# Where x tiles 4 to 7 land, the order of a first stage written out by hand, and context products two tiles later

## The chip, the cores and the metric

The kernel runs on one core of a Trainium2 chip. The metric is the device time of that core in microseconds (us), the median of several runs. The core has a matrix engine (PE, with its weight loads shown apart as PEld), a vector engine (DVE), a scalar engine (ACT), a general engine (POOL) and the queue SP, from which nearly all DMA transfers are issued here. Matmul results are written to PSUM, which this kernel uses as eight banks of 128x512 floats.

## The reference

One layer of an image backbone on 1024 latent tokens (x) and 256 context tokens (ctx), width 1024:

```
shift, scale, gate = adaln(c, w_ada, b_ada);  shift_c, scale_c, _ = adaln(c_ctx, ...)
h  = rmsnorm(x, norm_g)   * (1 + scale)   + shift
hc = rmsnorm(ctx, norm_g) * (1 + scale_c) + shift_c
q, k, v, za, u, bg, cg, zc = split(h @ w_in)          # 8 x 512 columns
kc, vc = split(hc @ w_in[:, 512:1536])
attn = neighbourhood_attention(rms(q), rms(k), v, rms(kc), vc, rpb) * silu(za)
conv = bg * conv3(cg * u) * silu(zc)
out  = x + gate * (concat(attn, conv) @ w_out)
```

All products are formed with an operand split into a high and a low float32r half: high*high, high*low, low*high.

## The kernel before

**Three places.** The kernel has a first stage (in the trace up to about 62 us on PE), a stage of 32 projection tiles (8 for each pair of heads, with context products and turns of the results between them), and then attention and output. The change touches the first stage and the first few tiles of the second.

**The first stage** is a list of short words, `LOADS` (line 36) and `STEPS` (lines 37 to 49), which `do` (line 789) runs in the order written. Up to the attention stage every engine's instructions, and SP's DMA issues, are chained in program order (`ordered`, lines 56 to 76), so a word that has to wait holds up all later words on its own engine. Since all of these instructions are issued in the helper, the profile gives nearly all of them line 71, and they are told apart by tile names. The words, with the engine that they run on:

- SP, loads: `s` a slab of the modulation weights (1 MB, three buffers), `t` a 128x512 piece of x transposed (256 KB; `t0k` for tokens 0 to 511 in three buffers, `t1k` for tokens 512 to 1023 in eight), `c` a weight chunk of the convolution columns and `q` one of the first pair of heads (192 KB; both in the five `wr` buffers), `x` a tile of 128 rows of x and `n` one of the two tiles of context tokens (512 KB), `e` context tokens transposed (`xc`), `g` the gains and the table for the rotations.
- PE: `pr k` the products of slab k with the conditioning vectors (64 small matmuls), `fc h k i` one of the three products of chunk k with token half h (three 128x512 matmuls, tile `acc`), `wb k` the products of the shift with chunk k (8 matmuls, tile `shifted`), `T t` two transposes of x tile t, `Rt g` transposes of the row sums of group g (into `tr`), `fill n` n matmuls with zeros.
- ACT: `ch`/`qh` the high half of a chunk, `sq t` the sum of squares of tile t, `p k` and `hi h k` high halves of the scaled tokens, `sh`, and `R g` the copy of `tr` into a spread row `rs`.
- DVE: `tp`, `ab` (modulation of slab k), `cl`/`ql` low halves of chunks, `m k`, `u h k` (scaling), `lo h k` low halves, `rp` (normalises an `acc` bank), `rg` (rotation tables), `wt` (transposes `shifted`), and with POOL `root g` (the inverse root of a group's sums; group 0 is x tiles 0 to 3, group 1 is 4 to 7, group 2 the context tiles).
- `conv` runs the next part of the first convolution group: a copy on ACT, a product on DVE, and the second time two more ACT additions.

There are 48 `fc` words; a slab's `pr k` comes ahead of `tp k`, `ab k`, and these ahead of `p1k`, `u0k` and all that follows for that k.

**x tiles** (`load_x`, line 564). Tiles 0 to 3 go into two places of the pool that later holds the h tiles 6 and 7 (`place(6)`, `place(7)`, two tiles in each). Tiles 4 to 7 and the two context tiles share two buffers `xn`.

**After the list** the first convolution group is finished on DVE (four taps and two gains, tile `cv`). Then the `rope` table goes out to `rope_d` and back (SP), POOL clears `gacc` (in the buffer that the taps read), SP loads one row into it, and then loads the first unit weights `uraw`. These four DMA steps are in this order on SP.

**The projection loop** (line 1190) runs n over the tiles. In turn n: PE does tile n (24 matmuls, tile `pacc`, banks in the order S, S, O, O of line 308, so tile 4 needs the bank of tile 0). Turn n measures tile n-1 (`head_scale`: ACT `sq`, DVE `ss`, POOL `ss`; `put_v`: ACT `vs`), and normalises tile n-2 (`rms_normed`: ACT `qn`, the last reader of that bank). `rotated` follows on DVE; every second turn PE turns two tiles (`turn_qk`: `trA`, `trB`). `CONTEXT` (line 50), 16 words that make the context operand `hc` on DVE and ACT, is issued in turn 0, right behind tile 0. At the end of turn 0 ACT makes the high halves `uh` of the unit weights (`do_acts`). At the end of turn `at` (line 1194), PE does the context products (`cacc`, 32 matmuls, in the two U banks); `ctx_sums` reads them in turn at+1, `normed_ctx` reads them for the last time in turn at+2 (ACT `kn`, `vs`), `turn_kc` is issued in turn at+3. From turn 5 on, 12 matmuls of the first unit (tile `pu`) follow behind each projection tile; their accumulator takes the first U bank too (`unit`, line 370: the tile is taken when its first matmul is issued).

Of the kernel before, what the change touches and what calls it, by code (L numbers as in the profile page):

```python
# [10 lines left out]
F32 = mybir.dt.float32  # L11
# [8 lines left out]
P = 128  # L20
D = 1024
# [4 lines left out]
NB = 8  # L26
NH, HD = 8, 64
NPAIR = NH // 2
# [4 lines left out]
TICKS = [2, 3, 3, 4, 4, 4, 4, 1] + [4, 4, 4, 1] + [4, 4, 4, 2] + [4, 4, 4, 1] + 3 * [4, 4, 3, 1] + [3, 2, 3, 1]  # L33
EPS = 1e-6

LOADS = "s0 t10 c0 x0 s1 t11 c1 x2 x3 x1 s2 c2 t12 t02"
STEPS = [
# [11 lines left out]
]  # L49
CONTEXT = "Hi0 Hi1 Lo0 Lo1 Hi2 Hi3 Lo2 Lo3 Hi4 Hi5 Lo4 Lo5 Hi6 Hi7 Lo6 Lo7"  # L50

# [4 lines left out]
def body(tc, es, x, xb, xt, cb_, ct, w_mod, w_gate, b_ada, w_grp, w_col, q_g, k_g, bias, w_out, vecs, cst, out):  # L56
# [86 lines left out]
    c2 = cp.tile([P, KT, 2], F32, name="c2")  # L143
# [10 lines left out]
    def place(k, shape, dtype, name):  # L154

        return hpool.tile(shape, dtype, name=name, tag=f"h{k}")

    def more_h(ks):
        for k in ks:
            t = place(k, [P, 2, T], F32R, f"h{k}")  # L160
            hh.append(t[:, 0])
            hl.append(t[:, 1])
# [10 lines left out]
    def chunk_load(col, k):  # L173
        raw = wpp.tile([P, 3, P], F32, name="wr", tag="wr", bufs=5)
        sp.dma_start(raw[:].rearrange("p a n -> p (a n)"), w_grp[NPAIR if col == CU else (col - CQ) // P, k])
        return raw
# [29 lines left out]
    def next_vs():  # L206
        vss.append(vss.pop(0))
        return vss[-1]
# [8 lines left out]
    def normed(qn, ps, scale, n):  # L217
        for h in range(n):
            cols = slice(h * HD, (h + 1) * HD)
            act.activation(qn[:, cols], ps[:, cols], AF.Identity, scale=scale[:, h:h + 1])  # L220
# [6 lines left out]
    def rms_normed(pp, ps, scale):  # L227

        qn = pp.tile([P, 256], F32, name="qn", tag="qn", bufs=3)
        normed(qn, ps, scale, 4)  # L230
        return qn
# [83 lines left out]
    def unit_load(col):  # L315
        raws = []
        for q in range(2):
            raws.append(uw.tile([P, 4, P], F32, name="uraw", tag="uraw", bufs=2))
            sp.dma_start(raws[q], w_col[col // P, :, 4 * q:4 * q + 4])
        return raws  # L320
# [85 lines left out]
    def z_col(f):  # L406
        return CZA + f * P if f < 4 else CZC + (f - 4) * P
# [154 lines left out]
    xn, xh, xc, slabs, mods, rows, chunks, pair = {}, {}, {}, {}, {}, {}, {}, []  # L562

    def load_x(t):
        if t < 4:
            if t % 2 == 0:
                pair.append(place(6 + t // 2, [P, 2, D], F32, "xn"))
            xn[t] = pair[t // 2][:, t % 2]
        else:
            xn[t] = xp.tile([P, D], F32, name="xn", tag="xn", bufs=2)[:]  # L570
        sp.dma_start(xn[t], xb[t * P:(t + 1) * P] if t < NB else cb_[(t - NB) * P:(t - NB + 1) * P])
# [189 lines left out]
    def keep_clock(n, late=False):  # L761

        v = zeros[:].rearrange("p (o n) -> p o n", o=1).broadcast_to([P, 4, P]) if late else warm
        ps = acc0[1][0][:].rearrange("p (a n) -> p a n", a=4) if late else acc0[1][0]
        for _ in range(n):
            pe.matmul(ps, zeros if late else warm[:, :P], v, start=True, stop=True)
# [22 lines left out]
    def do(steps):  # L789
        for word in steps.split():  # L790
            name = word.rstrip("0123456789")
            at = word[len(name):]
            does[name](*([int(at)] if name in ("warm", "fill") else map(int, at)))
# [9 lines left out]
    more_h(range(6))  # L803
    do(LOADS)
    keep_clock(6)
# [380 lines left out]
    def flush():  # L1186
        while stores:
            stores.pop(0)()

    for n in range(NT + 3):  # L1190


        p, t = divmod(n, NB)
        at = 2 if p < NPAIR - 1 else 0
        if t and p + 1 < NPAIR:
            raws.append(chunk_load(CQ + (p + 1) * P, t))
        if n == 0:
            loaded[z_col(4)] = unit_load(z_col(4))
        if n == NT - 8:
            loaded[z_col(0)] = unit_load(z_col(0))  # L1200
        if 9 <= n <= KT + 8:
            gate.load(n - 9)
        if n == NT - 3:
            act.activation(few[:, 5:6], ones, AF.Exp)
        if n == NT - 6:
            heads[0].masks()
            heads[0].load_k()
        if n == NT - 5:
            heads[0].load_q()
        flush()  # L1210
        blocks = divmod(n - 6, 5)
        if 6 <= n < 26 and blocks[1] == 0:
            load_blocks(blocks[0])
        if n == 24:
            sp.dma_start(ab[:, :, 0], g_d.rearrange("o (t p) -> p (o t)", p=P))

        if t == 0 and 0 < n < NT:
            nxt += map(chunk_split, raws)
            ch, nxt, raws = nxt, [], []
        if t == 0 and p + 1 < NPAIR:  # L1220
            raws.append(chunk_load(CQ + (p + 1) * P, 0))
        if n == 0:
            next(group0)
        if n == NT - 4:
            next(fill)
        if n < NT:
            tiles[n] = proj_tile(ch, t)
            if n == 0:
                do(CONTEXT)
        else:  # L1230
            for _ in range((4, 3, 1)[n - NT]):
                next(fill)
        if 5 <= n < 9:
            for _ in range(2):
                next(group0)
        if n == 9:
            for _ in group0:
                pass
        if 0 < n <= NT:
            scales[n - 1] = head_scale(pp, tiles[n - 1], 4)  # L1240
            if n % 2:
                vs = next_vs()
            put_v(vs, (n - 1) % 2, tiles[n - 1][:, 256:384])
            if n % 2 == 0:
                q, r = divmod(n - 1, NB)
                spill_v(q, r - 1, vs)
        if t == at + 1 and n < NT:
            ctx_sums(pp, cacc)
            cscales = [head_scale(pp, a, 2) for a in cacc]

        if 1 < n <= NT + 1:
            m, r = n - 2, (n - 2) % NB
            qn = rms_normed(pp, tiles[m], scales.pop(m))
        while waiting:
            waiting.pop(0)()
        if 4 <= t and p + 1 < NPAIR:
            nxt.append(chunk_split(raws.pop(0)))
        if 1 < n <= NT + 1:
            tiles[m] = rotated(pp, rope, qn, r)
        if t == at + 2 and n < NT:  # L1260
            kc = normed_ctx(pp, cacc, cscales)
        do_dves()
        if 6 <= n < 26 and blocks[1] in (2, 3):
            add_blocks(*blocks)
        if 10 <= n < KT + 10:
            gate.add(n - 10)
        do_acts()

        if n == KT + 11:
            gate.split()  # L1270
        if n == KT + 13:
            gate.sum()
        if t == at and n < NT:
            cacc = ctx_products(ch)
        if n % 2 == 0 and n >= 4:
            waiting.append(turn_qk(pp, (n - 4) // NB, [tiles.pop(n - 4), tiles.pop(n - 3)], (n - 4) % NB))
        if t == at + 3 and n < NT:
            waiting.append(turn_kc(pp, p, *kc))
# [74 lines left out]
    with sbuf("att") as ap, psum("psb") as psb:  # L1353
# [6 lines left out]
        for n in range(len(TICKS)):  # L1360
# [11 lines left out]
            if ready:  # L1372
                p = ready.pop()
# [83 lines left out]
    def four(tags):  # L1457
        return [bank("pout", tag) for tag in tags]
# [44 lines left out]
    m12, m22 = zip(*[(residual(c, 1), residual(4 + c, 1)) for c in every_tile])  # L1503
    load_left(6, "B")
    m11 = [residual(c, 0) for c in every_tile]
# [19 lines left out]
    c5 = four("OOUU")  # L1525
# [29 lines left out]
    c3 = four("OOUU")  # L1555
# [84 lines left out]
```

## Time and profile before

| what | us |
|---|---|
| median of 3 runs (lowest, highest) | 602.52 (602.45, 603.16) |
| the profiled execution's own time | 602.64 |
| its span, first to last instruction | 600.8 |
| PE busy in the span | 579.1 |
| DVE busy | 445.8 |
| ACT busy | 290.2 |

Every instruction row of the profile has its start in us, its length in us, the engine, the line (almost always the helper's line 71), the operation, and the tiles as output<-inputs; a row with x24 stands for 24 merged instructions. In square brackets stands the idle time of the engine just before the row, and what released it. Rows of the stretches (windows) have, for each engine, its busy time, the number of instructions, and then the granted clock of PE (PEclk, 1.00 is full speed), the busy share of the DMA engines and GB/s.

### The profile page before, as it was taken

How to read it: one execution, taken by the hardware profiler on the slowest of the kernel's cores; microseconds unless marked ns; L12 is line 12 of the kernel's file. 1: busy time of each engine (PE TensorE's matmuls, PEld its weight loads, DVE VectorE, ACT ScalarE, POOL GpSimd, SP SyncE). 2: the span in 40 equal slices, each digit the busy share in tenths (PEclk: the TensorE clock that was granted, in tenths of full speed). 3: DMA queues.
4: the chain of work that ended last, by engine and by line, in shares of the span. 5: the costliest groups of instructions: out<-in, count | busy, mean ns of one | idle time of the engine just before them, and what ended most of it. 6: DMA issues, size and time to landing. Idle time of an engine off the chain costs nothing.

```text
span 600.8 us, 10008 instructions
## 1 busy us (share of the span) xinstructions
PE 579.1 (96%) x3574; PEld 484.9 (81%) x3574; DVE 445.8 (74%) x894; ACT 290.2 (48%) x671; POOL 58.0 (10%) x83
## 2 busy tenths in 40 slices
PE   7899569999999999999999999999999999999998
PEld 4677469999999999988887777878787876888886
DVE  2556887356995765546898968898988887999952
ACT  4564546342553545543464446465644735643320
POOL 0000104112322223200000000000000001100000
PEclk9999879999999999999999999999999999999999
DMA  8988251537896879394616374736576363682632
GB/s 312 415 328 319 110 215 51 190 124 243 271 317 214 280 233 341 117 353 170 215 60 247 129 254 125 283 115 233 196 261 223 116 228 114 192 308 72 209 121 90
DMA packets 66678, 126.14 MB, mean 210 GB/s; under 512 B 8713, under 2 KB 27649, under 8 KB 64324
## 3 DMA queue, kind: packets, MB, share of 16 engines
q1 hardware_dynamic: 66244, 124.70, 59.3%
q0 software_dynamic: 384, 0.81, 0.5%
q8 instruction: 28, 0.46, 0.3%
q14 instruction: 22, 0.18, 0.1%
HBM read 92.38 MB, written 33.10 MB: 209 GB/s over the span
## 4 chain that ended last, share of the span: by engine, by line
PE 82%; DMA 8%; DVE 6%; ACT 2%; SPq 1%; issue 1%; DVEq 0%; ACTq 0%
PE pu L71 27%; PE pacc L71 19%; PE pout L71 13%; PE po L71 5%; PE cacc L71 4%; PE acc L71 3%; PE pss L71 3%; PE pc L71 2%; DMA slab<-in_w_mod 2%; PE pmx L71 2%; DMA xn<-in_cb 1%; PE trA L71 1%; DMA wr<-in_w_grp 1%; PE tr L71 1%; DMA y_d<-tb 1%
## 5 line engine op out<-in xcount | busy, mean ns | idle before, releaser
L71 PE MATMUL pu<-h,uh 128*128 128x512 f32 x544 | 174.3, 402 | 0.0
L71 PE MATMUL pacc<-w,h 128*128 128x384 f32 x768 | 141.9, 342 | 8.5 <-ACT rs L71 7.6
L71 PEld LDWEIGHTS pacc<-w,h 128*128 128x128 f32 x768 | 135.5, 192 | 9.3 <-ACT rs L71 7.9
L71 PEld LDWEIGHTS pu<-h,uh 128*128 128x128 f32 x544 | 97.4, 189 | 18.3 <-issue 1.2
L71 PE MATMUL pu<-h,ul 128*128 128x512 f32 x272 | 106.5, 392 | 0.0
L71 PE MATMUL pout<-right,left 128*128 128x512 f32 (+2 forms) x348 | 77.0, 383 | 0.0
L71 PEld LDWEIGHTS pout<-right,left 128*128 128x128 f32 x348 | 64.4, 188 | 12.7
L71 PEld LDWEIGHTS pu<-h,ul 128*128 128x128 f32 x272 | 51.1, 188 | 11.4
L71 POOL TENSOR_TENSOR ss<-ss,few 128x4 f32<-128x4 f32 (+1 forms) x40 | 41.3, 1033 | 128.1 <-DVE ss L71 127.7
L71 ACT COPY sc<-pc 128x512 f32<-128x512 f32 x32 | 18.7, 587 | 45.5 <-PE pc L71 45.5
L71 PE MATMUL acc<-h,w 128*128 128x512 f32 x144 | 36.4, 401 | 1.8 <-ACT h L71 1.7
L71 ACT ACTIVATE sq<-pacc 128x256 f32<-128x256 f32 x32 | 12.3, 385 | 48.7 <-PE pacc L71 48.2
L71 ACT ACTIVATE sc<-sc 128x512 f32<-128x512 f32 x32 | 20.3, 633 | 30.0 <-DVE sc L71 29.8
L71 PEld LDWEIGHTS acc<-h,w 128*128 128x128 f32 x144 | 26.0, 188 | 9.2 <-ACT h L71 2.6
L71 DVE TENSOR_TENSOR sum<-sum,sb 128x372 f32<-128x372 f32 (+2 forms) x64 | 31.1, 485 | 2.7
L71 DVE SCALAR_TENSOR_TENSOR m<-pout,ab,m 128x512 f32<-128x512 f32 (+2 forms) x34 | 22.9, 721 | 13.0 <-PE pout L71 12.9
L71 ACT ACTIVATE qn<-pacc,ss 128x64 f32<-128x64 f32 x128 | 30.0, 330 | 4.0 <-PE trA L71 2.5
L71 DVE TENSOR_TENSOR mx<-mx,sb 128x372 f32<-128x372 f32 (+2 forms) x64 | 30.9, 483 | 1.4
L71 DVE TENSOR_REDUCE ss<-sq 128x4 f32<-128x260 f32 (+1 forms) x40 | 15.7, 392 | 21.8 <-ACT sq L71 21.8
L71 DVE TENSOR_TENSOR sb<-pss,bt 128x192 f32<-128x192 f32 (+3 forms) x48 | 27.7, 604 | 4.2 <-PE pss L71 4.2
L71 DVE TENSOR_TENSOR ul<-uraw,uh 128x512 fp32r<-128x512 f32 x34 | 23.1, 685 | 10.0 <-ACT uh L71 10.0
L71 DVE TENSOR_TENSOR sb<-sb,mg 128x744 f32<-128x744 f32 (+2 forms) x32 | 26.7, 834 | 0.0
(154 smaller groups left out, 862.6 us busy)
## 6 DMA issues: line engine op xcount, KB each, us to landing
uraw<-in_w_col SPq DMA_DIRECT2D x34, 256.0 KB, 3.5
slab<-in_w_mod SPq DMA_DIRECT2D x8, 1024.0 KB, 10.3
q_d<-qs SPq DMA_DIRECT2D x32, 256.0 KB, 5.0
k_s<-k_d SPq DMA_DIRECT2D x8, 1024.0 KB
q_s<-q_d SPq DMA_DIRECT2D x16, 512.0 KB, 4.5
wr<-in_w_grp SPq DMA_DIRECT2D x40, 192.0 KB, 4.1
bt<-in_rpb SPq DMA_DIRECT2D x8, 564.0 KB, 8.3
xn<-in_xb SPq DMA_DIRECT2D x8, 512.0 KB
```

Of the source, the lines that this page charges most:

```text
L71: i = emit(*a, **kw)
```

## The change

- `load_x`: x tiles 4 to 7 go to the same two places as tiles 0 to 3 (tile 4 where tile 0 was, and so on). The two `xn` buffers are left to the context tiles alone.
- `LOADS` and `STEPS` have the same words, except that the zero matmuls are 1, 2 and 4 in place of 2 and 5, in another order. Among the differences: x0 to x3 are loaded behind the first two slabs; x4 and x5 are loaded around slab 4, x6 and x7 ahead of slab 5; the context tiles (`n0 n1`) are loaded ahead of slab 7, where they stood behind all slabs; `sq8 sq9 root2` come ahead of `pr7`, and `Rt2` and `R2`, which were among the last four words, stand well before the end of the list; `rg2 rg1` are the list's last words.
- `CONTEXT` is issued in turn 2, behind `rms_normed` of tile 0, and no longer in turn 0.
- For the first pair of heads the context products come at the end of turn 4 (behind tile 4) and no longer of turn 2. The other pairs keep theirs. With it `ctx_sums`, `normed_ctx` and `turn_kc` go to turns 5, 6 and 7.

```diff
-LOADS = "s0 t10 c0 x0 s1 t11 c1 x2 x3 x1 s2 c2 t12 t02"
+LOADS = "s0 t10 c0 s1 t11 c1 x0 x1 x2 x3 s2 c2 t12 t02"
 STEPS = [
-    "ch0 pr0 s3 t13 c3 t03 t14 c4 t04 tp0 ab0 p10 cl0 sh0 sq0 fc101 fc100 m10 fc102 pr1 s4 x4 x5 T0 ch1 wb0 tp1",
-    "ab1 cl1 p11 sh1 m11 fill2 fc110 sq2 sq3 fc111 fc112 sq1 root0 wb1 T3 ch2 T2 fill5 pr2 s5 tp2 ab2 cl2 sh2 p12",
-    "m12 T1 more Rt0 wb2 R0 fc120 fc121 v00 fc122 hi00 v01 u00 hi01 pr3 lo00 u01 lo01 u02 t05 t15 c5 fc000 fc002",
-    "fc010 tp3 hi02 ab3 fc001 ch3 fc012 p13 fc011 lo02 cl3 fc020 sh3 u03 fc022 hi03 ch4 fc021 m13 fc132 pr4 cl4",
-    "tp4 fc131 sq4 x6 ab4 lo03 fc130 u04 sh4 p14 fc031 fc140 sq5 x7 t16 s6 c6 t06 s7 t17 c7 t07 hi04 fc032 lo04",
-    "ch5 fc141 sq6 fc030 cl5 pr5 fc042 tp5 fc041 fc040 sh5 ab5 wb3 q0 p15 u05 fc151 hi05 sq7 m14 ch6 fc050 root1",
-    "fc150 lo05 m15 fc142 cl6 pr6 tp6 ab6 fc152 sh6 p16 u06 wb5 wb4 q1 q2 g0 n0 n1 m16 hi06 fc051 fc052 ch7 lo06",
-    "pr7 fc162 qh0 qh1 cl7 tp7 fc160 ql0 ab7 qh2 Rt1 fc161 ql1 p17 u07 sh7 wb6 q3 R1 hi07 ql2 u10 fc060 sq8 fc171",
-    "wb7 q4 q5 q7 q6 e0 e1 e2 e3 lo07 u11 fc062 hi10 m17 fc061 fc072 qh3 fc170 sq9 wt ql3 fc071 lo10 qh4 fc172",
-    "hi11 u12 ql4 rp0 root2 qh5 fc070 qh6 ql6 qh7 ql5 ql7 hi12 lo12 lo11 conv0 rp1 u13 u14 hi13 hi14 rg3 lo13 u15",
-    "lo14 hi15 u16 rg0 lo15 rp2 u17 rg2 rg1 hi17 conv0 lo17 Rt2 hi16 R2 lo16",
+    "pr0 s3 t13 c3 ch0 tp0 ab0 cl0 p10 m10 fc101 fc100 sh0 ch1 pr1 tp1 sh1 ab1 wb0 cl1 fc102 p11 m11 sq0 sq1",
+    "fill1 fc110 fc111 fc112 sq2 T1 fill2 T2 T0 x4 s4 t03 x5 t04 x6 c4 t14 sq3 ch2 fill4 pr2 root0 tp2 sh2 ab2",
+    "cl2 p12 wb1 Rt0 m12 T3 x7 s5 R0 v00 u00 wb2 hi00 v01 fc121 ch3 fc120 hi01 fc122 pr3 fc001 lo00 u01 sq4 tp3",
+    "fc000 sh3 lo01 fc002 u02 t05 t15 c5 s6 t16 c6 fc010 fc012 fc011 ab3 hi02 p13 fc020 lo02 fc022 m13 fc021 u03",
+    "t06 n0 n1 hi03 ch4 pr4 s7 c7 t17 cl3 tp4 lo03 fc130 sh4 fc132 ab4 fc030 p14 u04 t07 hi04 sq5 cl4 fc031 fc131",
+    "fc032 sq7 fc140 lo04 sq6 more m14 ch5 fc042 fc041 root1 pr5 fc141 tp5 sh5 fc142 wb3 q0 ab5 u05 p15 hi05 wb4",
+    "q2 cl5 pr6 m15 lo05 fc051 tp6 ch6 ab6 fc151 fc052 fc152 u06 sh6 p16 sq8 fc150 sq9 fc040 m16 fc160 fc050 hi06",
+    "cl6 wb5 q1 root2 pr7 fc161 ch7 lo06 tp7 ab7 sh7 Rt1 cl7 u07 p17 m17 qh0 fc162 wb7 wb6 q3 q4 qh2 R1 ql0 q5 g0",
+    "fc060 fc062 fc171 ql2 q6 u10 u12 qh1 ql1 q7 e0 e1 e2 e3 hi07 fc170 Rt2 lo07 fc172 fc061 fc070 hi10 fc071",
+    "lo10 qh3 ql3 qh5 qh4 ql4 R2 u11 qh6 ql5 hi12 ql6 hi11 qh7 fc072 lo12 wt ql7 lo11 rg0 u13 hi13 conv0 rp0 u14",
+    "hi14 rp1 lo13 u15 rp2 lo14 hi15 conv0 lo15 u16 u17 rg3 hi16 hi17 lo16 lo17 rg2 rg1",
 ]
...
-        if t < 4:
+        if t < NB:
             if t % 2 == 0:
-                pair.append(place(6 + t // 2, [P, 2, D], F32, "xn"))
+                pair.append(place(6 + t // 2 % 2, [P, 2, D], F32, "xn"))
...
-        at = 2 if p < NPAIR - 1 else 0
+        at = (4, 2, 2, 0, 0)[p]
...
             tiles[n] = proj_tile(ch, t)
-            if n == 0:
-                do(CONTEXT)
...
             qn = rms_normed(pp, tiles[m], scales.pop(m))
+        if n == 2:
+            do(CONTEXT)
```

## The prediction

> **What bounds the kernel now.** I read the page's engine table first, then PE's waits, then the timeline of each engine up to 112 us.
>
> ```profile
> PE 579.1 (96%) x3574; PEld 484.9 (81%) x3574; DVE 445.8 (74%) x894; ACT 290.2 (48%) x671; POOL 58.0 (10%) x83
> PE pacc L71 <- ACT rs L71: 7.6, 1, 7.6
> PE tr L71 <- POOL sums L71: 4.7, 1, 4.7
> PE tr L71 <- DMA slab<-in_w_mod: 1.0, 1, 1.0
> 50.60 1.10 PE L71 MATMUL tr<-slab,c 128*32 128x64 f32 x64
> 56.53 5.06 PE L71 MATMUL acc<-h,w 128*128 128x512 f32 x21
> 66.30 0.69 PE L71 MATMUL tr<-ci,sums 128*128 128x128 f32 x2 [4.72 <-POOL sums L71]
> 66.64 5.75 PE L71 MATMUL pacc<-w,h 128*128 128x384 f32 x24
> 79.98 10.06 PE L71 MATMUL pacc<-w,h 128*128 128x384 f32 x48 [7.58 <-ACT rs L71]
> 89.88 5.71 PE L71 MATMUL cacc<-w,hc 128*128 128x512 f32 x32
> 103.75 0.27 PE L71 MATMUL trA<-ci,rot 128*128 128x128 f32 x1
> ...
> 104.32 4.43 PE L71 MATMUL pacc<-w,h 128*128 128x384 f32 x24
> 108.59 0.63 PE L71 MATMUL pu<-h,uh 128*128 128x512 f32 x2
> ...
> 111.36 0.38 PE L71 MATMUL trC<-ci,kn 128*128 128x128 f32 x2
> 111.49 4.42 PE L71 MATMUL pacc<-w,h 128*128 128x384 f32 x24
> ...
> 66.00:68.00 2.00, 1.70 (x6) 1.70 (x7) 2.00 (x5) 0.45 (x1) 1.43 (x6) 0.54 0.00 0
> 80.00:82.00 2.00, 2.00 (x6) 2.00 (x7) 1.97 (x4) 1.38 (x2) 0.00 (x0) 0.50 0.47 197
> ```
>
> PE is the bound, and its two long idles lie at the seam of the stages: 4.72 us ahead of `Rt2`, and 7.58 us ahead of tile 1, which waits for `R2` to read the bank `tr`. After each the granted clock is about half (0.54, 0.50), so that tile 0 takes 5.75 us and tiles 1 and 2 together 10.06, against 4.43 for tile 5 (4.27 from its start to the first `pu`). That is 1.3 and 1.4 us more: 15.0 us at the seam in all. The page leaves PE 600.8-579.1 = 21.7 us of idle, 12.3 of them here. So what the change is worth is read at one point: **when PE starts tile 6**, now 111.49, or 111.36 (so 2.77 behind the first `pu`) without `trC`, which is issued later in the new order.
>
> **The change part by part.**
>
> *The loads.* x4 to x7 no longer wait for `sq4` and `sq5`, the context tiles come earlier, and slabs 5 and 7 stand behind 1.05 MB more.
>
> ```profile
> 20.00:30.00 10.00, 8.86 (x164) 6.75 (x165) 7.35 (x15) 5.28 (x10) 0.52 (x1) 1.00 1.04 417
> 36.00:38.00 2.00, 2.00 (x11) 1.64 (x10) 1.13 (x2) 2.00 (x4) 0.00 (x0) 1.00 0.64 245
> ...
> 40.00:50.00 10.00, 10.00 (x181) 7.48 (x181) 6.04 (x12) 5.56 (x11) 1.44 (x1) 1.00 0.95 358
> 33.91 4.05 SPq L71 DMA_DIRECT2D xn<-in_xb  x2
> 59.79 1.06 ACT L71 ACTIVATE xn<-xn 128x1024 f32<-128x1024 f32 x1 [3.71 <-DMA xn<-in_cb]
> 62.08 0.56 DVE L71 TENSOR_TENSOR w<-wr,w 128x384 fp32r<-128x384 f32 x1 [3.62 <-ACT w L71]
> ```
>
> The transfers run at some 417 GB/s, with a hole from 36 us on (245) where SP stood 4.05 us at x6 and x7. With the hole filled, the 18.25 MB up to slab 7 land near 49.5 us, before PE gets to `pr7`; I take no loss there, and none at slab 5. If they land 1 us late, `pr7` and all behind it are 1 us late. `sq8` no longer holds ACT for 3.71 us and with it DVE for 3.62: gained on DVE. The order of SP's queue costs something else, below.
>
> *PE's list.* Ahead of `pr7` stand one more `fc` (37 for 36; 5.06/7 = 0.72 us) and behind slab 2, for which PE waits (the row with slab) in both, `wb1` (8 small matmuls, an estimate of 0.4 at most from `pr7`'s 64 in 1.10). So `pr7` starts near 50.60+1.1 = 51.7 and ends at 52.8; the list ends about 62.3, with `Rt2` now inside it. Both idles as they are now go. What is late next?
>
> *DVE to the end of the list.* Behind `pr7` DVE has, by start-to-start steps:
>
> ```profile
> 51.81 0.24 DVE L71 STREAM_TRANSPOSE rw<-tr 128x64 f32<-128x64 f32 x1
> 65.14 1.49 DVE L71 TENSOR_TENSOR w<-wr,w 128x384 fp32r<-128x384 f32 x3
> 66.55 1.47 DVE L71 SCALAR_TENSOR_TENSOR h<-hw,b,h 128x512 fp32r<-128x512 f32 x2
> 76.48 1.29 DVE L71 TENSOR_TENSOR rg<-rw 128x512 f32<-128x512 f32 x2
> 79.06 0.69 DVE L71 TENSOR_TENSOR cu<-acc,ub 128x512 f32<-128x512 f32 x1 [1.29 <-ACT acc L71]
> ```
>
> 9 low chunk halves x 0.47 = 4.2; 9 `u`, 9 `lo` and `m17` x 0.66 = 12.5; 4 `rg`, 3 `rp`, 2 `conv` x 0.6 = 5.4; small ones 0.8: 22.9 us. Without any idle that ends at 75.7. Both `conv` copies stand behind a `hi` on ACT (1.2 us, as in the row at 79.06, and some 0.6), and `q6`, `q7` are issued behind `wb6`, `ql2`, `ql1` and the three `g0` loads, so near 59 us, and hold `ql6` and `ql7` for about 1.7. I take 3.5: **the list ends on DVE at E = 79.2**. With the idle that DVE has now (81.0-51.8-22.4 = 6.8) it would be 82.
>
> `wt` stands late in this list, and I take its bank `shifted` for that of tile 0: tile 0 starts near 64.5, tiles 0 to 3 end near 81.
>
> *Tile 4.* It needs the bank of tile 0, thus `qn` of tile 0 on ACT. Ahead of that in ACT's order stands `uh`, which waits for `uraw`, behind `gacc`, behind the taps. Now this chain is covered by `CONTEXT`, which comes first; the change puts `CONTEXT` behind it.
>
> ```profile
> 77.80 0.33 SPq L71 DMA_DIRECT2D rope_d<-rg  x1
> 81.64 0.32 SPq L71 DMA_DIRECT2D rope<-rope_d  x1
> 80.99 2.98 DVE L71 SCALAR_TENSOR_TENSOR cv<-cu,vecT,cv 128x512 f32<-128x512 f32 x4
> 84.09 0.96 POOL L71 MEMSET gacc<- 128x1024 f32 x1 [16.58 <-DVE cv L71]
> 85.38 0.81 SPq L71 DMA_DIRECT2D uraw<-in_w_col  x2
> DMA to landing us min/median/max: 2.8/2.8/2.8
> 85.09 0.87 DVE L71 SCALAR_TENSOR_TENSOR hw<-xc,ab,rs 128x256 f32<-128x256 f32 x2
> ...
> 91.72 0.88 DVE L71 SCALAR_TENSOR_TENSOR hc<-hw,b,hc 128x256 fp32r<-128x256 f32 x2 [0.18 <-ACT hc L71]
> 91.99 1.13 ACT L71 CAST uh<-uraw 128x512 fp32r<-128x512 f32 x2
> 95.45 0.93 ACT L71 ACTIVATE qn<-pacc,ss 128x64 f32<-128x64 f32 x4 [0.89 <-POOL ss L71]
> ```
>
> From the end of the list on DVE (now 80.99) to `uraw`'s issue is 4.39 us. The second `uraw` half is issued 0.4 later and lands after 2.8: E+7.6; `uh` 0.6; from its end (93.12) to `qn`'s (96.38) 3.26: E+11.5. But `rg1` is the last word now, so the 1 MB `rope` load (3.84 us behind `rope_d`) is issued at E+3.9, straight ahead of `uraw`. Its 1.05 MB at 417 GB/s are 2.5 us; behind these and a landing of 2.8 `uraw`'s second half is there near E+9.2, and `qn` ends at E+13.1. I take that: **tile 4 starts at 92.3**, after 11 us idle. The Trainium skill (DMA: Bandwidth & Descriptors, "Queues, rings and completion order") says that SP's DMAs use one row of rings and are consumed in ring order on each engine, which speaks for 13.1; shared evenly it would be E+11.5 to E+13, 1 us less.
>
> *Tile 4 to tile 6.* Tile 4 at half clock 4.3+1.4; `cacc` 5.6 (`CONTEXT`, 7.5 us from 85.09 to 92.6 now, starts when `qn` does and ends in time); turns 0.6 (103.75 to 104.32); tile 5 4.3: 16.2 us. Then `pu` takes the first U bank, which `cacc` holds until `normed_ctx` in turn 6.
>
> ```profile
> 102.34 0.61 ACT L71 ACTIVATE kn<-cacc,ss 128x64 f32<-128x64 f32 x2
> 102.74 0.36 ACT L71 COPY vs<-cacc 128x128 f32<-128x128 f32 x1
> ```
>
> Now that reader ends at 103.1, 7.5 us behind `cacc` (95.6), and `pu` comes at 108.6: hidden. In the new order ACT must first do `sq` and `vs` of tile 5, `qn` of tile 4 and a weight copy: not before 2.6 us behind tile 5 (rows like these). PE leaves only 0.6+4.3 = 4.9 us behind `cacc`, 7.5-4.9 = 2.6 by the present distance; with ACT's queue behind `CONTEXT` I count 4.7. I take 3.7, with 2.77 for `pu` itself, and no clock loss. The two idles in the first fence say that 4.7 us halves the clock; the Trainium skill (TensorE: Matmul & The Clock Gate, "What's actually happening") gives an idle window of about 3.4 us. By it the 3.7 us would cost up to 1.4 more; PE's waits hold no idle between 1.8 and 4.7 us here.
>
> Sum: 92.3+16.2+3.7+2.8 = 115.0, against 111.36: **3.6 us later**. Behind it PE is full as before, so 602.64+3.6 = 606.2 (the execution profiled lies 0.12 above the median): **606.2 us**.
>
> **The rivals.**
>
> 1. *The U bank doesn't hold `pu`*, or ACT has caught up by then. For it: PE idles 11 us ahead of tile 4, in which nothing else runs. Against: three readers in turns 5 and 6 stand behind tile 5's own `sq`. Tile 6 at 111.3: no change, 602.5, from 601 to 604 with E's bounds.
> 2. *Faster: DVE has no idle left.* Its place is E, its price one for one. With E = 75.7 and `uraw` landing after 2.8, tile 4 starts at 87.2, tile 6 at 109.9: 601.1, or 597.4 with rival 1. Break-even is a tile 4 start at 88.7, so E = 75.6 with the slow landing and 77.2 with the quick one. For it: the 3.62 us wait is gone and chunks land earlier. Against: the late `q6`, `q7` and ACT's strict order.
> 3. *Tile 4 isn't held at all*: all of 15.0 us is gained, 587.6. It needs `qn` of tile 0 before 81, with `uraw` there by 76; the `cv` and `gacc` rows speak against it.
> 4. *Slower still*: E = 82, 4.7 us at `pu` and a half clock behind it: +2.8+1.0+1.4, 611.4.
>
> **How the numbers follow.** Forecast (slower by 1.2 to 6 us) 0.50, rival 1 0.22, rival 2 0.13, rival 3 0.07, rival 4 0.08. What lies within 0.2% (1.2 us) can't be told from no change. Faster: 0.13+0.07 and 0.08 of rival 1, 0.28; same: 0.10 of rival 1 and 0.05 of the forecast's edge, 0.15; slower 0.57. The range reaches down over rival 1 and most of rival 2, 599.0, and up to 609.5; left out are rival 3 and the ends of 2 and 4. The forecast's own range is 603.8 to 609.
>
> **What would show it.** Right: no wait of PE for `sums` or `rs`; `xn<-in_cb` without an ACT wait; PE idle some 11 us near 81 with the releaser ACT `qn`; ACT waiting for the DMA of `uraw` ahead of `uh`; a PE wait ahead of the first `pu` released by ACT `vs`; tile 6 near 115. Wrong: tile 4 starting before 88.7, `pu` without a wait, or PE waiting for slabs 5 or 7.

## The result, and the profile after

| | before | after |
|---|---|---|
| median (lowest to highest of 4 runs), us | 602.84 (602.45 to 604.64) | 612.85 (611.98 to 613.41) |
| span of the profiled execution | 600.8 | 611.5 |
| PE busy / not busy in the span | 579.1 / 21.7 | 582.0 / 29.5 |
| PE starts tile 6 (before: without `trC`) | 111.36 | 121.89 |
| from there to the end of the span | 489.4 | 489.6 |

The ratio is 1.0159, with an interval from 1.0134 to 1.0184: the change makes the kernel slower by 1.6%. The forecast was 606.2, with a range up to 609.5. The sign holds, the size doesn't: tile 6 starts 10.5 us later, not 3.6, and from there to the end the two kernels differ by 0.2 us.

PE's waits in the changed kernel (us in total, times, longest). The waits for `sums` (4.7) and `rs` (7.6) are gone; three others are there. The last row, the wait for slab 2 near 20 us, was there before with 1.0:

```profile
PE pacc L71 <- ACT qn L71: 10.9, 1, 10.9
PE pacc L71 <- DVE wbT L71: 5.4, 1, 5.4
PE pu L71 <- ACT vs L71: 3.2, 1, 3.2
PE tr L71 <- DMA slab<-in_w_mod: 1.8, 1, 1.8
```

PE's timeline of the changed kernel:

```profile
51.99 1.08 PE L71 MATMUL tr<-slab,c 128*32 128x64 f32 x64
...
67.51 19.73 PE L71 MATMUL pacc<-w,h 128*128 128x384 f32 x96 [5.37 <-DVE wbT L71]
...
98.11 5.71 PE L71 MATMUL pacc<-w,h 128*128 128x384 f32 x24 [10.87 <-ACT qn L71]
103.66 5.71 PE L71 MATMUL cacc<-w,hc 128*128 128x512 f32 x32
...
109.78 4.43 PE L71 MATMUL pacc<-w,h 128*128 128x384 f32 x24
...
117.45 0.78 PE L71 MATMUL pu<-h,uh 128*128 128x512 f32 x2 [3.24 <-ACT vs L71]
...
121.89 4.35 PE L71 MATMUL pacc<-w,h 128*128 128x384 f32 x24
```

Read it from the bottom. The first unit, from 117.45 to 121.89, takes 4.44 us where it took 2.77 before, behind a wait of 3.24. Tile 4 stood 10.87 us. Tiles 0 to 3 (the row x96) start behind 5.37 us of idle, up to 73 us at half clock (0.50), and that costs nothing by itself, because tile 4 waits for something else anyway (an experiment below shows it).

That something is on ACT. Its timeline in the changed kernel:

```profile
65.34 0.51 ACT L71 CAST w<-wr 128x384 fp32r<-128x384 f32 x1 [4.59 <-DMA wr<-in_w_grp]
...
93.60 1.19 ACT L71 CAST uh<-uraw 128x512 fp32r<-128x512 f32 x2 [10.89 <-DMA uraw<-in_w_col]
...
97.12 0.93 ACT L71 ACTIVATE qn<-pacc,ss 128x64 f32<-128x64 f32 x4 [0.89 <-POOL ss L71]
...
117.02 0.38 ACT L71 COPY vs<-cacc 128x128 f32<-128x128 f32 x1
```

ACT stands 10.89 us at `uh`, and `qn`, which frees the bank for tile 4, stands behind it. The last row is the reader that PE's first `pu` waits for. The first row is the surprise: 4.59 us for a weight chunk of the first pair of heads. It holds DVE too, as DVE's timeline and its row of a window, 53.00 to the first tap of `cv`, show:

```profile
65.88 0.56 DVE L71 TENSOR_TENSOR w<-wr,w 128x384 fp32r<-128x384 f32 x1 [3.68 <-ACT w L71]
...
83.48 3.05 DVE L71 SCALAR_TENSOR_TENSOR cv<-cu,vecT,cv 128x512 f32<-128x512 f32 x4
```

```profile
53.00:83.48 30.48, 23.48 (x41) 0.89 0.29 94
```

So the list ends on DVE at 83.48, after 23.48 us of work and 7.0 of idle. The late chunk is `q6`. Its transfer is in SP's timeline of the changed kernel (start and length of the issue), and the time from its issue to its landing in the view of the tile `wr` behind it:

```profile
56.85 0.42 SPq L71 DMA_DIRECT2D rw<-in_q_norm_g  x1
57.32 0.42 SPq L71 DMA_DIRECT2D rw<-in_k_norm_g  x1
57.79 0.43 SPq L71 DMA_DIRECT2D rw<-in_cst  x1
58.32 2.19 SPq L71 DMA_DIRECT2D wr<-in_w_grp  x2
...
83.59 0.33 SPq L71 DMA_DIRECT2D rope_d<-rg  x1
...
87.81 0.32 SPq L71 DMA_DIRECT2D rope<-rope_d  x1
...
88.54 0.81 SPq L71 DMA_DIRECT2D uraw<-in_w_col  x2
```

```profile
DMA to landing us min/median/max: 7.0/7.0/7.0
```

`q6` was issued at 58.32, close to the "near 59 us" of the prediction, but ACT got it at 65.34, 7.0 us behind the issue. Windows of the changed kernel show what the DMA engines did meanwhile (the last two numbers are their busy share and GB/s):

```profile
59.00:60.00 1.00, 1.00 (x6) 0.81 (x5) 1.00 (x2) 0.45 (x2) 0.00 (x0) 1.00 0.06 17
60.00:61.00 1.00, 1.00 (x6) 0.84 (x5) 0.51 (x3) 0.75 (x3) 0.00 (x0) 1.00 0.19 66
...
118.00:120.00 2.00, 2.00 (x6) 1.60 (x5) 1.42 (x4) 0.00 (x0) 1.77 (x3) 0.50 0.97 302
```

They were all but idle, at 17 and 66 GB/s, with a chunk waiting in the queue. Ahead of it stand the three loads of `g0`, of which the first two put one row of 256 bytes into each of 128 partitions (the third, 512 KB, is the table). The last row gives the clock behind the 3.24 us of idle: 0.50.

### The profile page after: what moved, and what is told of

It reads as the page before. It is cut to its first block, busy times and chain, and to the rows that moved or that the text cites. A ratio compares the mean times of both kernels' runs of the same rounds, so it can differ in the third digit from the quotient of the medians.

```text
span 611.5 us, 10013 instructions
## 1 busy us (share of the span) xinstructions
PE 582.0 (95%) x3574; PEld 488.4 (80%) x3574; DVE 445.3 (73%) x894; ACT 290.9 (48%) x671; POOL 56.7 (9%) x83
## 4 chain that ended last, share of the span: by engine, by line
PE 77%; DMA 9%; DVE 7%; ACT 3%; issue 3%; SPq 1%; POOL 0%; DVEq 0%; ACTq 0%; POOLq 0%
PE pu L71 27%; PE pacc L71 15%; PE pout L71 13%; PE po L71 5%; PE acc L71 4%; PE pss L71 3%; PE cacc L71 3%; PE pc L71 2%; DMA slab<-in_w_mod 2%; DMA wr<-in_w_grp 2%; PE pmx L71 2%; PE tr L71 1%; PE trA L71 1%; DMA rs_d<-sums 1%; DVE hw L71 1%
## 5 line engine op out<-in xcount | busy, mean ns | idle before, releaser
L71 DVE SCALAR_TENSOR_TENSOR m<-pout,ab,m 128x512 f32<-128x512 f32 (+2 forms) x34 | 22.9, 719 | 13.0 <-PE pout L71 12.9
```

What stands on the lines that cost most here:

```text
L71: i = emit(*a, **kw)
```

## The experiments

Each is timed against the kernel before on the same chip; the medians of before lay there between 603.71 and 604.22. The traces are single executions, and in those with the new order `pr7` starts at 51.99 (the changed kernel) and anywhere from 50.74 (run 5) to 52.29 (run 10), also where nothing ahead of it was touched (51.12 in run 6). So up to some 1.3 us of a difference between two traces can be there before the stretch in question begins; where it matters, times are counted from `pr7`. The theory on record (A) is that of the prediction: tile 4 is held by `uraw` through ACT, then `pu` by the bank that `cacc` holds. To it came, from the profile after, G: the list's late end on DVE comes from the loads of `g0` ahead of `q6`.

**1. The new order alone** (`e1_order_only`): loads, list and places as after, the loop as before.

```diff
-        at = (4, 2, 2, 0, 0)[p]
+        at = 2 if p < NPAIR - 1 else 0
...
+            if n == 0:
+                do(CONTEXT)
...
-        if n == 2:
-            do(CONTEXT)
```

> The new loads, order and places of x, with the loop of before (CONTEXT in turn 0, context products at the end of turn 2). Theory A (the loss comes from three holds that the loop's two edits open: unit weights ahead of tile 0's measuring on ACT, the U bank at the first unit, and a late list end that delays the first of them): with CONTEXT back in front, uraw's landing is covered again; the list ends on DVE 2.5 us later than before (83.5 against 81.0), so CONTEXT ends near 95 and tile 6 starts near 112 to 114: 603.5 to 605.5. Rival B (the new order of the first stage is what costs): near 611 to 613, as the changed kernel.

Measured 603.25, just under A's range, ratio 0.9985 (0.9974 to 0.9997). PE's timeline of this run:

```profile
67.03 15.44 PE L71 MATMUL pacc<-w,h 128*128 128x384 f32 x72 [5.04 <-DVE wbT L71]
...
88.23 8.20 PE L71 MATMUL cacc<-w,hc 128*128 128x512 f32 x32 [5.76 <-ACT hc L71]
```

Here is where the gain at the seam goes: the 4.7 and 7.6 us of idle are gone, but PE waits 5.04 for `wt`'s bank, then 5.76 for the context operand, and runs behind both at a lower clock (`cacc` 8.20 instead of 5.71). `CONTEXT`, in its old place, covers `uraw`; there is no hold at tile 4. By itself the new order moves the wait and no more.

**2. The new loop alone** (`e2_loop_only`): the old order, with `CONTEXT` in turn 2 and `at` 4.

> The loads, order and places of before, with the loop of the change (CONTEXT in turn 2, context products at the end of turn 4). Theory A: the list ends on DVE at 81.0 and uraw lands near 88.5, so qn of tile 0 ends near 92.6, about when tile 3 does; tile 4 is hardly held, but the first unit waits 3 us for the U bank and runs at half clock behind it: tile 6 near 116 to 117, 607 to 608.5. Rival B: the loop costs nothing or gains, 602 to 603.

Measured 609.1, ratio 1.0077 (1.0056 to 1.0098), 0.6 us above A's range. PE's timeline:

```profile
80.61 19.23 PE L71 MATMUL pacc<-w,h 128*128 128x384 f32 x96 [6.71 <-ACT rs L71]
...
113.23 1.22 PE L71 MATMUL pu<-h,uh 128*128 128x512 f32 x2 [3.00 <-ACT vs L71]
117.56 4.33 PE L71 MATMUL pacc<-w,h 128*128 128x384 f32 x24
```

The wait at `pu` comes with the loop, whatever the order: 3.00 us, and the 12 products take 4.33. PE has no wait for `qn` here, because tiles 1 to 4 (the row x96) start only at 80.61, behind the old wait for `rs`. So the hold at tile 4 belongs to neither half alone: it takes the order that brings tiles 1 to 3 early, and the loop that takes `CONTEXT` out of `uraw`'s way. The parts' ratios (0.9985, 1.0077) don't make the whole's (1.0159).

**3. `uh` two turns later** (`e3_uh_late`): the changed kernel, with ACT's weight casts from the end of turn 2 on and none in turns 0 and 1, so `qn` of tile 0 no longer stands behind `uraw`.

```diff
-        do_acts()
+        if n > 1:
+            do_acts()
```

> The changed kernel, with the high halves of the first unit's weights made on ACT from turn 2 on, not in turn 0. Theory A: tile 0's measuring no longer waits for uraw; qn of tile 0 ends near 90.5 to 91, tile 4 starts 7 us earlier than 98.1, the first unit still waits for the U bank: 605 to 606.5. Rival C (the wait for uraw hides another limit, DVE's backlog, so that tile 4 comes late anyway): 610 to 613.

Measured 604.88, just under A's range, ratio 1.001 (0.9994 to 1.0025). PE's timeline:

```profile
89.74 6.68 PE L71 MATMUL pacc<-w,h 128*128 128x384 f32 x24 [4.08 <-ACT qn L71]
...
109.50 0.74 PE L71 MATMUL pu<-h,uh 128*128 128x512 f32 x2 [2.67 <-ACT vs L71]
112.39 4.35 PE L71 MATMUL pacc<-w,h 128*128 128x384 f32 x24
```

Tile 4 starts 8.4 us earlier, tile 6 9.5; 0.6 of each is there at `pr7` already (51.41). The hold through ACT's order is shown, and its price. The remainder of the gain is at `pu`: behind 2.67 us of idle its 12 products take 2.89.

**4. The first unit a turn later** (`e4_unit_a_turn_later`): the changed kernel, units behind tiles 6 to 9 in place of 5 to 8, so that `normed_ctx` is through.

```diff
-        if 5 <= n < 9:
+        if 6 <= n < 10:
...
-        if n == 9:
+        if n == 10:
```

> The changed kernel, with the first unit's products in turns 6 to 9, not 5 to 8. Theory A: the U bank is free by then, the 3.2 us wait and the half clock behind it (4.4 us for twelve products in place of 2.8) go: 607.5 to 608.5. Rival D (PE only meets the same late ACT one tile further on, or the clock falls anyway): 611 to 613.

Measured 608.67, just over A's range, ratio 1.0064 (1.0041 to 1.0087). PE's timeline:

```profile
97.40 6.92 PE L71 MATMUL pacc<-w,h 128*128 128x384 f32 x24 [11.30 <-ACT qn L71]
...
110.29 8.59 PE L71 MATMUL pacc<-w,h 128*128 128x384 f32 x48
```

Tiles 5 and 6 run in one piece, 8.59 us for both, with no wait for `vs`. The hold at tile 4 stays (11.30). The bank is the second cost, independent of the first.

**5. The gains loaded early** (`e5_gains_early`): the changed kernel, `g0` moved from behind `q5` to behind `t07`, and so issued from 43.96 us on in place of 56.85.

```diff
-    "t06 n0 n1 hi03 ch4 pr4 s7 c7 t17 cl3 tp4 lo03 fc130 sh4 fc132 ab4 fc030 p14 u04 t07 hi04 sq5 cl4 fc031 fc131",
+    "t06 n0 n1 hi03 ch4 pr4 s7 c7 t17 cl3 tp4 lo03 fc130 sh4 fc132 ab4 fc030 p14 u04 t07 g0 hi04 sq5 cl4 fc031 fc131",
...
-    "cl6 wb5 q1 root2 pr7 fc161 ch7 lo06 tp7 ab7 sh7 Rt1 cl7 u07 p17 m17 qh0 fc162 wb7 wb6 q3 q4 qh2 R1 ql0 q5 g0",
+    "cl6 wb5 q1 root2 pr7 fc161 ch7 lo06 tp7 ab7 sh7 Rt1 cl7 u07 p17 m17 qh0 fc162 wb7 wb6 q3 q4 qh2 R1 ql0 q5",
```

> The changed kernel, with the three loads of g0 (two of them 128 rows of 256 bytes) issued behind t07, not ahead of q6 and q7. Theory G (the two small-row loads keep the DMA engines at some 15 to 40 GB/s for 5 us, and q6, queued behind them, lands 7 us after its issue; that holds qh6 on ACT 4.6 us and so the list's end on DVE): q6 lands some 3 us after its issue, no long ACT wait for a chunk, the list ends on DVE near 79.5 to 80 in place of 83.5, and all behind follows one for one: 608.5 to 609.5. Rival H (q6 and q7 are late because their buffers come free late, at wb6, ql2 and ql1): the list ends at 82.5 or later, 611.5 to 613.

Measured 608.34, just under G's range, ratio 1.0062 (1.004 to 1.0085). The last weight chunk, `q7`, now lands 2.5 us behind its issue, by the view of `wr`, and DVE's wait for chunks falls from 4.2 us to 0.9. DVE's timeline, then PE's:

```profile
78.66 3.05 DVE L71 SCALAR_TENSOR_TENSOR cv<-cu,vecT,cv 128x512 f32<-128x512 f32 x4
```

```profile
62.87 16.94 PE L71 MATMUL pacc<-w,h 128*128 128x384 f32 x96 [1.97 <-DVE wbT L71]
...
112.80 0.74 PE L71 MATMUL pu<-h,uh 128*128 128x512 f32 x2 [3.02 <-ACT vs L71]
...
117.26 4.35 PE L71 MATMUL pacc<-w,h 128*128 128x384 f32 x24
```

The list ends on DVE 4.8 us earlier and tile 6 starts 4.6 earlier; counted from `pr7`, which was 1.25 earlier in this trace, it is 3.6 and 3.4. Either way it is one for one, as the prediction priced E. The expectation has the DMA engines at 15 to 40 GB/s for 5 us; the windows of the changed kernel show 17 and 66 GB/s, for about two.

**6. `wt` early** (`e6_wt_early`): the changed kernel, `wt` moved ahead of `qh3 ql3`, so that tile 0 doesn't wait for it.

```diff
-    "lo10 qh3 ql3 qh5 qh4 ql4 R2 u11 qh6 ql5 hi12 ql6 hi11 qh7 fc072 lo12 wt ql7 lo11 rg0 u13 hi13 conv0 rp0 u14",
+    "lo10 wt qh3 ql3 qh5 qh4 ql4 R2 u11 qh6 ql5 hi12 ql6 hi11 qh7 fc072 lo12 ql7 lo11 rg0 u13 hi13 conv0 rp0 u14",
```

> The changed kernel, with wt (the last reader of the bank of tile 0) moved ahead of ql3 on DVE. Theory A: PE's wait of 5.4 us ahead of tile 0 shrinks, but tile 4 still waits for qn of tile 0, so the same time turns up ahead of tile 4: 612 to 613.5, no change. Rival I (the wait for wt is part of the loss): 608 to 610.

Measured 611.31, ratio 1.0119 (1.0088 to 1.015), an interval that overlaps the changed kernel's and misses both expectations. PE's timeline:

```profile
98.01 6.61 PE L71 MATMUL pacc<-w,h 128*128 128x384 f32 x24 [17.34 <-ACT qn L71]
...
117.45 0.73 PE L71 MATMUL pu<-h,uh 128*128 128x512 f32 x2 [2.43 <-ACT vs L71]
```

The 5.37 us at tile 0 aren't gained: they reappear in the wait at tile 4 (17.34 for 10.87), which starts at 98.01 for 98.11. So `wt` is off the path as long as tile 4 is held. The 1.5 us that may be gained come from the clock: the 12 products behind 2.43 us of idle take 2.86.

**7. The four edits together** (`e7_all_four`: those of runs 3, 4, 5 and 6).

> The changed kernel with the four edits together: gains early, wt early, high halves of the unit weights from turn 2, first unit from turn 6. Theory A with G: the list ends on DVE near 80, qn of tile 0 near 87, no wait at the first unit: tile 6 (less the 2.8 us of products that now come behind it) some 6 us earlier than with the high halves late alone: 598 to 600, faster than the kernel before. Rival C (DVE's work to the end of CONTEXT is the bound in any order): 602 to 604.

Measured 596.93, ratio 0.9876 (0.9847 to 0.9905): faster than before by 1.2%, and better than expected by 1.1 us at least. PE's timeline:

```profile
85.72 7.19 PE L71 MATMUL pacc<-w,h 128*128 128x384 f32 x24 [7.48 <-ACT qn L71]
...
98.87 8.59 PE L71 MATMUL pacc<-w,h 128*128 128x384 f32 x48
```

Tile 0 starts at 61.40 in one piece with the list; a hold of 7.48 us at tile 4 is what is left.

**8 and 9. The early gains without the new loop** (`e8_order_only_gains_early`: run 1 with run 5's edit; `e9_before_gains_early`: the kernel before, with `g0` behind `t07`).

> The new order with the loop of before, and the gains' loads early. Theory G: CONTEXT and with it the context products end some 3.5 us earlier than with the new order alone: 599.5 to 600.5. Rival H: 602.5 to 603.5.

> The kernel before, with the three loads of g0 issued behind t07, not ahead of the context tiles. Theory G (the two small-row loads hold up whatever is queued behind them, here the context tiles that land 7.6 us after their issue and hold ACT 3.7 us): ACT's wait for in_cb goes, DVE's list end comes 3 to 4 us earlier, and with it R2 and tile 1: 598.5 to 600. Rival J (the context tiles are late for another reason, or the list's end doesn't move): 602 to 603.5.

Run 8 measured 599.13, just under G's range, ratio 0.9915 (0.9887 to 0.9944): `cacc` starts at 84.54 instead of 88.23, of which 0.8 is there at `pr7`. A row of PE's timeline shows the clock after a short idle (the last section comes back to it):

```profile
63.53 14.32 PE L71 MATMUL pacc<-w,h 128*128 128x384 f32 x72 [2.36 <-DVE wbT L71]
```

Run 7, timed beside it on the same chip, is 2.2 us faster still, with no overlap (595.91 to 597.1 against 598.82 to 599.38). It differs from run 8 by the new loop with the edits of runs 3 and 4, and by `wt` early, so what the loop alone is worth can't be told from these two. Run 9 measured 605.39, ratio 1.0026 (1.0013 to 1.004), and missed both of its ranges: ACT's timeline, then PE's:

```profile
56.95 1.56 ACT L71 CAST w<-wr 128x384 fp32r<-128x384 f32 x3 [4.73 <-DMA wr<-in_w_grp]
```

```profile
82.67 10.06 PE L71 MATMUL pacc<-w,h 128*128 128x384 f32 x48 [9.04 <-ACT rs L71]
```

In the old order the context tiles no longer wait, but now it is `q0`, `q1` and `q2` that stand behind `g0` in SP's queue and come 4.73 us late; the wait for `sums` shrinks from 4.72 to 0.74, but a new one of 3.09 (for ACT's `h`) stands ahead of it, the wait for `rs` grows from 7.58 to 9.04, and tile 1 starts 2.7 us later (82.67 for 79.98). Here moving the loads only moved the gap. It costs little where nothing that is needed soon stands next in the queue, as in run 5, where ACT waits 1.43 us for an earlier chunk.

**10. The context products at turn 3** (`e10_all_four_at_3`: run 7 with `at` 3 for the first pair).

> The version with all four edits, and the context products at the end of turn 3, so ahead of tile 4 and its wait for qn of tile 0. Theory A: PE does the context products while CONTEXT still runs (from about 87 on, to its end near 92.5 plus one step), and tile 4 follows without a wait: about 1 us earlier than with turn 4, 595 to 596.5. Rival K (the products then wait step by step for CONTEXT and tile 4 ends no earlier): 596.5 to 598.

Measured 599.66, ratio 0.993 (0.9916 to 0.9944), above both ranges, and 2.7 us slower than run 7. PE's timeline:

```profile
86.62 7.87 PE L71 MATMUL cacc<-w,hc 128*128 128x512 f32 x32 [7.51 <-ACT hc L71]
...
99.06 8.59 PE L71 MATMUL pacc<-w,h 128*128 128x384 f32 x48
...
113.02 0.41 PE L71 MATMUL trC<-ci,kn 128*128 128x128 f32 x2 [1.94 <-DVE qs L71]
```

The products stand right behind `CONTEXT` and wait 7.51 us for it in place of tile 4's 7.48; tile 5 starts at 99.06 for 98.87, or 0.7 us earlier if counted from `pr7` (52.29 here, 51.41 in run 7). A new wait comes behind: `turn_kc` now falls into a turn in which `turn_qk` also turns, and PE waits 1.94 us ahead of `trC`. That the two share banks is read from the code, not tested.

**11. Only the two small-row loads early** (`e11_gain_rows_early`): the changed kernel, the two gain loads behind `t07`, the table (512 KB in long rows) left ahead of `q6` and `q7`.

> The changed kernel, with only the two small-row loads of g0 (128 rows of 256 bytes each) issued behind t07; the 512 KB table stays where it was, ahead of q6 and q7. Theory G1 (the two small-row loads are what holds the queue): as with all three moved, 608 to 609.5, the list's end on DVE near 79 to 80. Rival G2 (the table's 512 KB ahead of q6 are what holds it): 611.5 to 613, the end near 83.

Measured 609.55, just over G1's range, ratio 1.0081 (1.005 to 1.0113). DVE's timeline, then ACT's at `q6`, then PE's:

```profile
80.83 3.05 DVE L71 SCALAR_TENSOR_TENSOR cv<-cu,vecT,cv 128x512 f32<-128x512 f32 x4
```

```profile
62.69 0.51 ACT L71 CAST w<-wr 128x384 fp32r<-128x384 f32 x1 [1.54 <-DMA wr<-in_w_grp]
```

```profile
64.86 16.92 PE L71 MATMUL pacc<-w,h 128*128 128x384 f32 x96 [2.93 <-DVE wbT L71]
```

E comes 2.65 us earlier with the two rows moved, and 4.8 with all three loads; counted from `pr7` (51.77 here, 50.74 in run 5) it is 2.4 and 3.6. So the two small loads, 64 KB of the 576, are the larger part; the table, in order ahead of the chunk, is the other 1.1 or so. `q6` says the same: issued at 57.16 behind the table alone, it reaches ACT 5.5 us later, in place of 7.0 behind all three. E lies between the values of the two theories: both kinds of load count. The PE row is for the clock, in the last section.

## Why the prediction was right in kind and wrong in size

Each line is a step of the sum, at the point where PE starts tile 6.

| step | predicted | measured | off by |
|---|---|---|---|
| list ends on DVE (E) | 79.2 | 83.48 | +4.3 |
| E to the start of tile 4 | 13.1 | 14.6 | +1.5 |
| tile 4 to the end of tile 5 | 16.2 | 16.1 | -0.1 |
| wait of the first `pu` | 3.7 | 3.2 | -0.5 |
| the 12 `pu` products | 2.77 | 4.44 | +1.7 |
| tile 6 starts | 115.0 | 121.9 | +6.9 |

**The loads and PE's list.** Right: `pr7` started at 51.99 (forecast 51.7; other runs of this order have it from 50.74 to 52.29), no wait at slabs 5 or 7, none for `sums` or `rs`, no ACT wait for the context tiles. Tile 0 came at 67.51 for 64.5, and run 6 shows that this costs nothing here.

**E, the main error.** The working put DVE at 22.9 us of work and 3.5 of idle. DVE's waits in the changed kernel, from the first rows behind `pr7` to E, say where it fell:

```profile
DVE w L71 <- ACT w L71: 4.2, 2, 3.7
...
DVE cu L71 <- ACT ub L71: 1.3, 1, 1.3
DVE cu L71 <- ACT acc L71: 1.2, 1, 1.2
```

Of the 4.3 us, 2.5 are the wait for the chunks: 4.2 where I had "about 1.7". The rest is small: the two `conv` waits are 2.5 where I had 1.8, the work is 0.6 longer, and start and other idle make 0.5. The step that failed is thus the term for `q6` and `q7`. I had seen that `q6` and `q7` are issued behind the three `g0` loads, and priced only the order of the issues, with a landing as quick as others; the landing was 7.0 us. With `g0` moved (run 5) the wait for chunks falls to 0.9 and E, counted from `pr7`, comes 3.6 us earlier. (I also took DVE's idle before for 6.8 us; DVE is busy for 22.96 of the 29.18 us from 51.81 to 80.99, so it is 6.2, which leaves the 82 as it is.) The trace of before held the warning. Its context tiles too were queued behind `g0`, and the 3.71 us wait for them, which I counted as a gain of the change, was the same gap, here in the windows of before:

```profile
52.00:54.00 2.00, 2.00 (x12) 1.68 (x11) 0.79 (x4) 1.27 (x3) 0.00 (x0) 1.00 0.19 51
```

51 GB/s with 1 MB in the queue is not a stretch in which nothing was asked for. The second of the two small loads itself took 6.9 us there from its issue to its landing. The change gave the wait to the next in line, and run 9 shows it passing to whatever is queued there instead.

**E to tile 4.** The mechanism was right, link by link (runs 1 and 3). `uraw` landed 5.0 us behind its issue at 88.54, and the `rope` load ahead of it was itself 4.2 us behind `rope_d` in place of 3.8; my working had the second half there at E+9.2, and `uh` began at E+10.1 and ended at E+11.3. The Trainium skill (DMA: Bandwidth & Descriptors, "Queues, rings and completion order") has SP's transfers consumed in ring order; the 5.0 us behind 1 MB, against 2.8 where `rope` was issued 3.7 us ahead (before), agree. Run 2 agrees as well: in its old order `rope` is issued 3.7 us ahead of `uraw`, and `uraw` lands after 2.9. No run changed that alone, so this cause of the 1.5 us is supported, not shown.

**`pu`.** The wait was foreseen to half a microsecond, and runs 2 and 4 show its cause. "No clock loss" was wrong: 4.44 us at a clock of 0.50. What the forecast set aside, up to 1.4 us for an idle of 3.7, came at 3.24, with 1.7.

**The rivals.** Rival 4, "slower still", at 611.4, is nearest: E beyond 82 and a half clock at `pu`. I gave it 0.08, as if both were mishaps, where the trace of before had rows for each. Its nearness is in part luck: its 4.7 us at `pu` was too much, and the 1.5 us at `uraw` aren't in it. Rivals 1 and 2 fall: the bank did hold `pu`, and with `g0` moved early E was still 78.7, above the 75.6 to 77.2 that rival 2 needs. Rival 3 was not met by the change, but run 3 shows that more than half of the hold at tile 4 was one line of ACT's order.

## What to carry to other kernels

When a load that was waited for is moved, ask what stood ahead of it in its queue, and who is next there now: the wait may not belong to the load. When a step is taken out of an engine's in-order list, look at what it covered: here the context operand hid a transfer, and behind that transfer stood the operation that frees a bank. And price an order as a whole, since two halves that cost nothing and 0.8% cost 1.6% together; the same change with four small corrections was 1.2% faster than before.

## What the runs showed of the hardware

- **Loads of short rows hold up what is queued behind them.** Behind two loads of 128 rows of 256 bytes and the 512 KB table, a 192 KB load landed 7.0 us after its issue (after); behind the table alone 5.5 (run 11); with none of the three just ahead, the next such load landed after 2.5 (run 5). For some 2 of the 7.0 us the DMA engines moved 17 to 66 GB/s. The Trainium skill (DMA: Bandwidth & Descriptors, "Specifications") wants at least 512 bytes for full rate; the runs agree that these loads are far from it, and add that what is queued behind them waits too. Why the engines were busy for only 6 and 19% of that time, no run shows.
- **An idle of 2.4 to 3 us may or may not halve the clock.** The 12 `pu` products took 2.86 us behind 2.43 of idle (run 6) and 2.89 behind 2.67 (run 3), but 4.33 behind 3.00 (run 2), 4.46 behind 3.02 (run 5) and 4.44 behind 3.24 (after). That looks like a limit near 3 us, but two other rows speak against one: the projection tiles of run 8 ran at 0.50 from 64 to 67 us behind only 2.36 of idle (72 matmuls in 14.32 us), and those of run 11 at 1.00 behind 2.93 (96 in 16.92). So the length of the idle alone doesn't decide it here. The Trainium skill (TensorE: Matmul & The Clock Gate, "What's actually happening") gives a window of about 3.4 us that runs freely; the same page, "Why this matters for your kernels", warns of gaps beyond about 3 us. Neither figure is a safe limit in these runs: 2.36 us was enough once. A window that runs freely would make it matter when an idle falls as well as how long it is; no run here tests that.
